# Four edits around an RWKV scan: the block inverse emitted ahead of its quarter, Gram products of both halves at once, the root of the first norm in PSUM, more filling ahead of chunk 0

## The chip, the cores and the metric

One core of a Trainium2 chip runs the whole program in one launch. TensorE (PE) does matrix products, VectorE (DVE), ScalarE (ACT) and GpSimd (POOL) do elementwise work, SyncE (SP) issues the transfers. The metric is device time in microseconds, the median of several executions.

## The reference

A trunk of two layers over 1024 tokens of width 1024, in float32. Layer 0 is an RMSNorm, one wide projection whose columns go to an RWKV-7 time mixer (8 heads of 64) and to chunked attention (8 heads of 64), gates, an output projection and a residual. Layer 1 is an RMSNorm, a projection, a gated position mixer and an output projection. A last RMSNorm follows. The part that the change touches most is the time mixer:

```python
def step(state, inp):
    r_t, w_t, k_t, v_t, a_t, b_t = inp
    sa = jnp.einsum('bhvk,bhk->bhv', state, a_t)
    state = (state * w_t[:, :, None, :]
             + sa[..., None] * b_t[:, :, None, :]
             + v_t[..., None] * k_t[:, :, None, :])
    y_t = jnp.einsum('bhvk,bhk->bhv', state, r_t)
    return state, y_t
...
y_a = rwkv7_mix(...) * jax.nn.silu(gate_a)
y_b = chunk_attention(q_b, k_b, v_b, att_bias) * jax.nn.silu(gate_b)
return h + jnp.concatenate([y_a, y_b], axis=-1) @ w_out
```

## The kernel before

A float32 product is done as three products of split operands (`mm3`, lines 262, 264, 266: high by high, high by low, low by high), which is the great bulk of TensorE's work; the high and low parts of the normed input are xH and xL, those of the weights wh and wl.

The stages in time:

- **Head** (to 36 us). x is loaded in eight tiles of 128 tokens, in two halves of four. `square` sums the squares; `scale0` forms the root with `rsqrt_act` (lines 89 to 93: reciprocal, square root on ScalarE, then three VectorE steps on tiles of four or two columns, in batches of 4, 2 and 2 tiles of x per half) and scales the tiles xt; `norm_t` transposes them (L305) and evicts xH (L307, ScalarE) and xL (L308, VectorE). GpSimd meanwhile makes the weights' low parts (L231). `lora_evac` follows the first projection and runs a Tanh (L452, with a load of ScalarE's function table) and two copies.
- **Projections** of the time mixer (36 to 255 us). They write ar, bk and v, the operands of the scan, to DRAM (`ar_d`, `bk_d`, `v_d`).
- **Scan** (about 263 to 560 us). 1024 tokens are 16 chunks of 64, in four quarters of four. `stage_a(q)` loads a quarter's operands (L691, L693, L696), forms the Gram products of keys and receptances per chunk and head (tile psg, L712), masks them into G and ag (L718, VectorE), scales bk (L675, GpSimd) and transposes it (pst, L681). A head pair stands in 128 partitions, head h in half h. `stage_b(q)` inverts the quarter's unit triangular blocks: four 32-wide transposes on VectorE (nw, L742), 15 times two small VectorE steps (L753, L755) on blocks of 16, and then four sets of 32-wide products on TensorE (psx, L771) with copies between, the last of them into G (L790). `stage_c(q)` runs the chain over chunks: zz and yy (L815, L818), copy z (L822), us (L825), copies uv (L828), us (L831), sum into the next chunk's uv (L836), yy (L838). `stage_d(q)` is the group norm of the result, with transposes psy (L872), and its store.
- **Filling.** Attention's projections (q, k, v, gate) are a generator of single matmuls. `fill.pump(n, mark, low)` emits n of them at a lowered priority, not ahead of the instruction mark. `QP`, `QB` and `QC` say how many go where: QP ahead of the first Gram product, QB[0] beside the first inverse, QB[q+1] between quarters, QC inside chunks. Their results leave by `split_evac` (tile hl, stored to q_d and k_d) and `vb_evac`.
- **Attention** (560 to 790 us), with the time mixer's output projection as filling (`out_steps`: residual tile res, loaded at L1135 from a pool of two buffers, summed at L1142, stored to hp_d at L1167), then attention's own half of the output projection.
- **Layer 1 and the last norm** (790 us to the end).

The order on every engine is set by the scheduler of the tile framework: it takes instructions by priority, which falls with the order of emission, and by its own estimate of readiness; `tc.add_manual_dep(..., sched_only)` adds an order without a semaphore. Within an engine everything then runs in that order.

Of the kernel before, what the change touches and what calls it, by code (L numbers as in the profile page):

```python
# [8 lines left out]
F32 = mybir.dt.float32  # L9
# [3 lines left out]
AF = mybir.ActivationFunctionType  # L13
# [39 lines left out]
YP = 1  # L53
LATE = 1
NPO = 1
QP = 44
FILLS = [5, 4, 4, 6, 4, 3, 3, 3]
QA = 14
QB = [80, 28, 16, 30]
QC = [[8, 8, 7], [8, 9, 7], [8, 8, 9], [8, 8, 7]]  # L60
W0SCALE = 0.6065306597126334

# [5 lines left out]
def rsqrt_small(nc, pool, out, v, tag):  # L68

    shp = list(v.shape)  # L70
    t = pool.tile(shp, F32, tag=tag, name="rsq_t")
    nc.vector.tensor_single_scalar(out.bitcast(I32), v.bitcast(I32), 1, op=ALU.arith_shift_right)
    nc.vector.tensor_scalar(out.bitcast(I32), out.bitcast(I32), -1, 0x5F3759DF, op0=ALU.mult, op1=ALU.add)
    if shp[1] == 1:
        h = pool.tile(shp, F32, tag=tag + "h", name="rsq_h")
        nc.vector.tensor_single_scalar(h, v, -0.5, op=ALU.mult)
    for _ in range(3):
        if shp[1] == 1:
            nc.vector.scalar_tensor_tensor(t, out, h, out, op0=ALU.mult, op1=ALU.mult)
        else:  # L80
            nc.vector.tensor_mul(t, out, out)
            nc.vector.scalar_tensor_tensor(t, t, -0.5, v, op0=ALU.mult, op1=ALU.mult)
        nc.vector.scalar_tensor_tensor(out, t, 1.5, out, op0=ALU.add, op1=ALU.mult)


def rsqrt_act(nc, pool, out, v):

    t = pool.tile(list(v.shape), F32, tag="rsqa", name="rsqa", bufs=2)
    nc.vector.reciprocal(t, v)
    nc.scalar.activation(out, t, AF.Sqrt)  # L90
    nc.vector.tensor_tensor(t, out, out, op=ALU.mult)
    nc.vector.scalar_tensor_tensor(t, t, -0.5, v, op0=ALU.mult, op1=ALU.mult)
    nc.vector.scalar_tensor_tensor(out, t, 1.5, out, op0=ALU.add, op1=ALU.mult)


@with_exitstack
def trunk_kernel(
# [13 lines left out]

    ident = cp.tile([P, P], F32, name="ident")
    make_identity(nc, ident)

    gmask = cp.tile([P, P], F32, name="gmask")
    nc.vector.memset(gmask, 1.0)
    for r in range(2):
        for q in range(2):
            blk = gmask[64 * r:64 * r + 64, 64 * q:64 * q + 64]
            nc.gpsimd.affine_select(  # L120
                out=blk, in_=blk, compare_op=ALU.is_ge, fill=0.0,
                base=-1 if q == 0 else 0, pattern=[[1, 64]], channel_multiplier=-1)
# [77 lines left out]
    def dtile(name, shape):  # L200
        return dr.tile(shape, F32, name=name)

    ya_d = dtile("ya_d", [NPAIR, P, T])
    yb_d = dtile("yb_d", [NPAIR, P, T])
    ar_d = dtile("ar_d", [NPAIR, P, 16, P])
    bk_d = dtile("bk_d", [NPAIR, P, 16, P])
    v_d = dtile("v_d", [NPAIR, T, P])
# [151 lines left out]
    def scale0(hf):  # L359
        for b in range(0, 4, BT[hf]):  # L360
            ts_ = range(4 * hf + b, 4 * hf + b + BT[hf])
            for t in ts_:
                square(t)
            bs = slice(ts_[0], ts_[-1] + 1)
            if any(SQ0[t] == "h" for t in ts_):
                nc.vector.tensor_tensor(ssq[:, 0, bs], ssq[:, 0, bs], ssq[:, 1, bs], op=ALU.add)
            nc.vector.tensor_scalar(ssq[:, 0, bs], ssq[:, 0, bs], 1.0 / D, 1e-6, op0=ALU.mult, op1=ALU.add)
            rsqrt_act(nc, p0, rstd[:, bs], ssq[:, 0, bs])
            for t in ts_:
                h_ = {"a": 1.0, "v": 0.0, "h": SPL}[SCL[t]]  # L370
                n_ = int(D * h_)
                if n_:
                    nc.scalar.mul(xt0[t][:, 0:n_], xt0[t][:, 0:n_], rstd[:, t:t + 1])
                if n_ < D:
                    nc.vector.tensor_scalar_mul(xt0[t][:, n_:D], xt0[t][:, n_:D], rstd[:, t:t + 1])
# [72 lines left out]
    def lora_evac(ps, hf):  # L448
        sh_wad(ps, hf)
        sl = slice(hf * 512, hf * 512 + 512)  # L450
        w, a = wad[hf][0:64], wad[hf][64:128]
        nc.scalar.activation(w, w, AF.Tanh)  # L452
        nc.scalar.copy(xw[0:64, sl], w)
        nc.scalar.copy(xa[64:128, sl], a)
# [90 lines left out]
    for p in range(NPAIR):  # L545
# [23 lines left out]
        for hf in range(2):  # L569
# [37 lines left out]
            nc.vector.tensor_tensor(kn, kn, ta, op=ALU.mult)  # L607
            nc.vector.tensor_tensor(bk[:, :, 0:64], c3(kn), c3(em), op=ALU.mult)
            nc.gpsimd.tensor_tensor(bk[:, :, 64:128], c3(km), c3(em), op=ALU.mult)
            nc.sync.dma_start(ar_d[p][:, 8 * hf:8 * hf + 8], ar)  # L610
            store_halves(bk_d[p][:, 8 * hf:8 * hf + 8], bk)
            def bonus(p=p, hf=hf, km=km, r=r, v=v, tsl=tsl):

                nc.vector.scalar_tensor_tensor(km, km, hrk[:, p:p + 1], r, op0=ALU.mult, op1=ALU.mult)
# [49 lines left out]
    def stage_a(q):  # L664
# [19 lines left out]
        for cg in range(2):  # L684
            o = 4 * q + 2 * cg
            uv = rq.tile([P, 2, 4, P], F32, tag="uv", name="uv", bufs=2)

            ag = rq.tile([P, 2, 4, 2, P], F32, tag="ag", name="ag", bufs=2)
            bk = (rb if q == 0 and cg else re_).tile(
                [P, 4, 2, P], F32, tag="bt" if q == 0 and cg else "bk", name="bk", bufs=2 if q == 0 and cg else 1)  # L690
            nc.sync.dma_start(bk, bk_d[:, :, o:o + 2, :].rearrange("a p c t -> p a c t"))  # L691
            for h in range(2):
                nc.sync.dma_start(ag[hss[h], h], ar_d[:, hss[h], o:o + 2, :].rearrange("a p c t -> p a c t"))  # L693
            for i in range(2):
                for h in range(2):
                    nc.sync.dma_start(  # L696
                        uv[oss[h], i, :, hss[h]],
                        v_d[:, 64 * (o + i):64 * (o + i) + 64, hss[h]].rearrange("a s n -> s a n"))
                    if q == cg == i == 0:
                        nc.gpsimd.memset(uv[hss[h], i, :, hss[h]], 0.0)  # L700
            if cg == 0:
                d["G"] = rq.tile([P, 2, 4, 2, P], F32, tag="G", name="G", bufs=1)
            g = d["G"][:, cg]
            bt = rq.tile([P, 4, 2, P], F32, tag="bt", name="bt", bufs=2)
            for pj in range(2):

                psg = [ps_m.tile([P, 4, P], F32, tag="m", name=f"psg{r}") for r in range(2)]
                for j in range(2):
                    for i in range(2):
                        for r in range(2):  # L710
                            for h in range(2):
                                nc.tensor.matmul(  # L712
                                    psg[r][(hss, oss)[r][h], 2 * j + i], lhsT=bk[hss[h], 2 * pj + j, i, (hss, oss)[r][h]],
                                    rhs=ag[hss[h], h, 2 * pj + j, i, :], start=True, stop=True)
                for dst, ps, r in ((g[:, 2 * pj:2 * pj + 2], psg[0], slice(0, P)),
                                   (ag[:, 0, 2 * pj:2 * pj + 2], psg[1], oss[0]),
                                   (ag[:, 1, 2 * pj:2 * pj + 2], psg[1], oss[1])):
                    nc.vector.tensor_tensor(  # L718
                        dst[r].rearrange("p j i t -> p (j i) t"), ps[r],
                        gmask[r].unsqueeze(1).to_broadcast([r.stop - r.start, 4, P]), op=ALU.mult)  # L720
# [395 lines left out]
    def out_steps(t, ps_o, src, k0, parts, resid, ht, hp, yp, yb_, hi=nc.scalar.copy, lo=nc.vector):  # L1116
# [81 lines left out]
    with tc.tile_pool(name="oh", bufs=1, reuse_waits="tile") as oh, \  # L1198
            tc.tile_pool(name="ps_ot", bufs=2, space=PSUM, reuse_waits="tile") as ps_ot:
        xss = []  # L1200
        for t in range(8):
# [185 lines left out]
```

## Time and profile before

| | us |
|---|---|
| median of 3 runs | 1215.05 (1209.55 to 1216.36) |
| the profiled execution | 1213.46 |
| its span, first to last instruction | 1211.7 |
| TensorE busy | 1132.9 (93%) |
| VectorE busy | 617.1 (51%) |
| ScalarE busy | 469.6 (39%) |
| GpSimd busy | 431.7 (36%) |
| mean granted TensorE clock | 0.962 of full speed |

The busy times are sums over a span of several stages with different limits, so each stage is read for itself. A row of the view by stretches gives, after the stretch and its length, the busy time of each engine with its count of instructions. In a row of the timeline the first number is the start, the second the time covered, xN the number of instructions run together, and the bracket says how long the engine stood idle before and what released it. A float32 matmul on TensorE leaves two records in the trace where the program has one instruction, so the trace counts 512 records of psg where the order has 256.

### The profile page before, as it was taken

To read this page: it belongs to the slowest core of one execution; us is meant where nothing else is said; L and a number is where in the kernel's file an instruction comes from. 1 tells how busy PE (TensorE), PEld (TensorE's weight loads), DVE (VectorE), ACT (ScalarE), POOL (GpSimd) and SP (SyncE) were. 2 spreads that over 40 slices of the span, in tenths; PEclk is the share of its full clock that TensorE was granted. 3 is DMA by queue.
4 is the path that set the end of the run, shared out by engine and by line. 5 is a ranking of instruction groups with operands and counts; after the bars stand their busy time and mean duration, and the time that the engine had idled before them with its cause. 6 is when DMAs were issued, how large, how long until landed. Compare 5 with 4: busy or idle time off the path is not lost.

```text
span 1211.7 us, 21587 instructions
## 1 busy us (share of the span) xinstructions
PE 1132.9 (93%) x8418; PEld 934.0 (77%) x8418; DVE 617.1 (51%) x1261; ACT 469.6 (39%) x1008; POOL 431.7 (36%) x447
## 2 busy tenths in 40 slices
PE   7899999979899798999998898799999999999997
PEld 4787778757767576777786777679999888888886
DVE  6555556547657649343677657265200463323443
ACT  5545554531323132223566645134425432221322
POOL 4335445342223323333322462311311464342232
PEclk8899999998999897999999899899999999999999
DMA  6115345477224441375577794764311132222542
GB/s 204 37 53 140 100 144 152 148 210 180 89 71 124 116 129 38 105 181 160 151 200 190 203 253 148 221 226 140 96 45 53 62 105 79 70 85 68 170 139 78
DMA packets 169127, 156.43 MB, mean 129 GB/s; under 512 B 25257, under 2 KB 138562, under 8 KB 168898
## 3 DMA queue, kind: packets, MB, share of 16 engines
q1 hardware_dynamic: 169026, 155.06, 43.8%
q8 instruction: 66, 1.08, 0.4%
q14 instruction: 35, 0.29, 0.1%
HBM read 102.02 MB, written 53.00 MB: 128 GB/s over the span
## 4 chain that ended last, share of the span: by engine, by line
PE 74%; DVE 11%; DMA 8%; issue 2%; ACT 2%; POOL 1%; SPq 1%; DVEq 0%; POOLq 0%; ACTq 0%
PE acc L262 13%; PE acc L264 13%; PE acc L266 13%; PE accv L262 3%; PE accv L264 3%; PE accv L266 3%; PE accu L262 2%; PE accu L264 2%; PE accu L266 2%; PE accg L262 2%; PE accg L266 2%; PE accg L264 2%; DMA res<-in_x_dram 1%; DVE nw L742 1%; PE st L1069 1%
## 5 line engine op out<-in xcount | busy, mean ns | idle before, releaser
L262 PE MATMUL acc<-xH,wh 128*128 128x512 f32 x528 | 215.1, 408 | 2.4 <-ACT xH L307 1.8
L264 PE MATMUL acc<-xL,wh 128*128 128x512 f32 x528 | 213.0, 404 | 0.0
L266 PE MATMUL acc<-xH,wl 128*128 128x512 f32 x528 | 211.8, 401 | 0.0
L231 POOL TENSOR_TENSOR wl<-wraw,wh 128x512 fp32r<-128x512 f32 (+1 forms) x106 | 149.4, 1429 | 166.0 <-ACT wh L228 156.0
L262 PEld LDWEIGHTS acc<-xH,wh 128*128 128x128 f32 x528 | 101.6, 192 | 24.6 <-ACT xH L307 2.2
L264 PEld LDWEIGHTS acc<-xL,wh 128*128 128x128 f32 x528 | 101.4, 192 | 21.6 <-issue 1.9
L266 PEld LDWEIGHTS acc<-xH,wl 128*128 128x128 f32 x528 | 101.1, 192 | 21.0 <-issue 0.3
L262 PE MATMUL acc<-WHL,yh 128*128 128x512 f32 x256 | 103.8, 405 | 13.0 <-DVE res L1142 7.2
L266 PE MATMUL acc<-WHL,yl 128*128 128x512 f32 x256 | 102.9, 402 | 0.0
L264 PE MATMUL acc<-WHL,yh 128*128 128x512 f32 x256 | 102.4, 400 | 0.0
L228 ACT CAST wh<-wraw 128x512 fp32r<-128x512 f32 (+1 forms) x102 | 62.4, 651 | 99.3 <-PE acc L264 38.3
L262 PE MATMUL accv<-wh,xH 128*128 128x256 f32 x256 | 72.2, 283 | 0.0
L264 PE MATMUL accv<-wl,xH 128*128 128x256 f32 x256 | 72.0, 283 | 0.0
L266 PE MATMUL accv<-wh,xL 128*128 128x256 f32 x256 | 71.6, 284 | 0.0
L262 PEld LDWEIGHTS acc<-WHL,yh 128*128 128x128 f32 x256 | 49.6, 194 | 24.2 <-issue 5.7
L266 PEld LDWEIGHTS acc<-WHL,yl 128*128 128x128 f32 x256 | 49.4, 193 | 10.4
L264 PEld LDWEIGHTS acc<-WHL,yh 128*128 128x128 f32 x256 | 49.6, 194 | 9.5
L1114 POOL TENSOR_TENSOR WHL<-wraw,WHL 128x512 fp32r<-128x512 f32 (+1 forms) x20 | 30.2, 1508 | 60.3 <-ACT WHL L1113 57.2
L262 PE MATMUL accu<-xH,wh 128*128 128x512 f32 x128 | 50.5, 395 | 0.0
L266 PE MATMUL accu<-xH,wl 128*128 128x512 f32 x128 | 49.9, 390 | 0.0
L264 PE MATMUL accu<-xL,wh 128*128 128x512 f32 x128 | 49.9, 390 | 0.0
L266 PE MATMUL accg<-xH,wl 128*128 128x512 f32 x128 | 49.9, 389 | 0.0
(430 smaller groups left out, 2463.8 us busy)
## 6 DMA issues: line engine op xcount, KB each, us to landing
wraw<-in_w_in_e_dram SPq DMA_DIRECT2D x66, 256.0 KB
wraw<-in_w_in_o_dram SPq DMA_DIRECT2D x32, 256.0 KB
xt<-in_x_dram SPq DMA_DIRECT2D x8, 512.0 KB
ar_d<-ar SPq DMA_DIRECT2D x8, 512.0 KB
q_d<-hl SPq DMA_DIRECT2D x8, 512.0 KB
bk<-bk_d SPq DMA_DIRECT2D x8, 512.0 KB
ag<-ar_d SPq DMA_DIRECT2D x16, 256.0 KB
bg<-bg_d SPq DMA_DIRECT2D x8, 512.0 KB
```

The costliest lines, as they stand in the source:

```text
L228: c_ = hi(wh[:, ks], raw)
L231: nc.gpsimd.tensor_tensor(wl[:, ks], raw, f32(wh[:, ks]), op=ALU.subtract)
L262: fill(nc.tensor.matmul(ps, lhsT=ah(k), rhs=bh(k), start=(k == 0), stop=False), k == 0)
L264: fill(nc.tensor.matmul(ps, lhsT=ah(k), rhs=bl(k), start=False, stop=False), False)
L266: fill(nc.tensor.matmul(ps, lhsT=al(k), rhs=bh(k), start=False, stop=(k == nk - 1)), False)
L742: mark = nc.vector.transpose(flat(nw[rs_]), g[rs_, :, o:o + 32].rearrange("p q (x t) -> p t x q", x=2))
L1069: nc.tensor.transpose(st[:, o:o + P], pfs[j][:, k0:k0 + P], ident)
L1114: (lo or (nc.vector if k % 2 else nc.gpsimd)).tensor_tensor(wl, raw, f32(wh), op=ALU.subtract)
```

## The change

1. `QP` goes from 44 to 84, `QB` from 80, 28, 16, 30 to 80, 10, 10, 10.
2. In the loop over quarters `stage_b(q + 1)` is emitted ahead of `stage_c(q)`, and the filling between quarters is tied to `stage_c`'s last copy.
3. The Gram product multiplies both 64-column halves of bk at once: 128 output partitions for one half of the input rows, so 8 instructions where 16 stood, in a tile psg for each input half. The masks become four of 64 partitions where one of 128 and two of 64 stood.
4. `rsqrt_act` can put the square root's result into PSUM, and its steps are arranged so that each reads the root from there; the head's batches do so. `rsqrt_small` for one column takes its operands as scalars by pointer.
5. The Tanh and two copies of `lora_evac` are ordered behind the eviction of xH that was emitted last.
6. `ar_d`, `bk_d` and `v_d` become two DRAM tiles each, one for each half of the tokens; the mask gmask is built by GpSimd just ahead of the scan; `res` has three buffers; the norm between the layers (`rms_scale`) takes its small tiles from another pool.

```diff
-QP = 44
+QP = 84
-QB = [80, 28, 16, 30]
+QB = [80, 10, 10, 10]
...
         if shp[1] == 1:
-            nc.vector.scalar_tensor_tensor(t, out, h, out, op0=ALU.mult, op1=ALU.mult)
+            nc.vector.tensor_scalar(t, out, h, out, op0=ALU.mult, op1=ALU.mult)
+            nc.vector.tensor_scalar(out, t, 1.5, out, op0=ALU.add, op1=ALU.mult)
...
-def rsqrt_act(nc, pool, out, v):
+def rsqrt_act(nc, pool, out, v, y=None):
     t = pool.tile(list(v.shape), F32, tag="rsqa", name="rsqa", bufs=2)
+    y = out if y is None else y
     nc.vector.reciprocal(t, v)
-    nc.scalar.activation(out, t, AF.Sqrt)
-    nc.vector.tensor_tensor(t, out, out, op=ALU.mult)
-    nc.vector.scalar_tensor_tensor(t, t, -0.5, v, op0=ALU.mult, op1=ALU.mult)
-    nc.vector.scalar_tensor_tensor(out, t, 1.5, out, op0=ALU.add, op1=ALU.mult)
+    nc.scalar.activation(y, t, AF.Sqrt)
+    nc.vector.scalar_tensor_tensor(t, v, -0.5, y, op0=ALU.mult, op1=ALU.mult)
+    nc.vector.tensor_tensor(t, t, y, op=ALU.mult)
+    nc.vector.scalar_tensor_tensor(out, t, 1.5, y, op0=ALU.add, op1=ALU.mult)
...
-            rsqrt_act(nc, p0, rstd[:, bs], ssq[:, 0, bs])
+            rsqrt_act(nc, p0, rstd[:, bs], ssq[:, 0, bs], ps_m.tile([P, BT[hf]], F32, tag="m", name="rsqp"))
...
-        nc.scalar.activation(w, w, AF.Tanh)
-        nc.scalar.copy(xw[0:64, sl], w)
-        nc.scalar.copy(xa[64:128, sl], a)
+        for i_ in (nc.scalar.activation(w, w, AF.Tanh), nc.scalar.copy(xw[0:64, sl], w),
+                   nc.scalar.copy(xa[64:128, sl], a)):
+            tc.add_manual_dep(i_.ins, evs[-1][0].ins.name, sched_only, reason="issue order")
...
-            nc.sync.dma_start(ar_d[p][:, 8 * hf:8 * hf + 8], ar)
-            store_halves(bk_d[p][:, 8 * hf:8 * hf + 8], bk)
+            nc.sync.dma_start(ar_d[hf][p], ar)
+            store_halves(bk_d[hf][p], bk)
...
-                psg = [ps_m.tile([P, 4, P], F32, tag="m", name=f"psg{r}") for r in range(2)]
+                psg = [ps_m.tile([P, 4, P], F32, tag="m", name=f"psg{h}") for h in range(2)]
                 for j in range(2):
                     for i in range(2):
-                        for r in range(2):
-                            for h in range(2):
-                                nc.tensor.matmul(
-                                    psg[r][(hss, oss)[r][h], 2 * j + i], lhsT=bk[hss[h], 2 * pj + j, i, (hss, oss)[r][h]],
-                                    rhs=ag[hss[h], h, 2 * pj + j, i, :], start=True, stop=True)
-                for dst, ps, r in ((g[:, 2 * pj:2 * pj + 2], psg[0], slice(0, P)),
-                                   (ag[:, 0, 2 * pj:2 * pj + 2], psg[1], oss[0]),
-                                   (ag[:, 1, 2 * pj:2 * pj + 2], psg[1], oss[1])):
-                    nc.vector.tensor_tensor(
-                        dst[r].rearrange("p j i t -> p (j i) t"), ps[r],
-                        gmask[r].unsqueeze(1).to_broadcast([r.stop - r.start, 4, P]), op=ALU.mult)
+                        for h in range(2):
+                            nc.tensor.matmul(psg[h][:, 2 * j + i], lhsT=bk[hss[h], 2 * pj + j, i, :],
+                                             rhs=ag[hss[h], h, 2 * pj + j, i, :], start=True, stop=True)
+                for h in range(2):
+                    for dst, r in ((g[:, 2 * pj:2 * pj + 2], hss[h]), (ag[:, h, 2 * pj:2 * pj + 2], oss[h])):
+                        nc.vector.tensor_tensor(
+                            dst[r].rearrange("p j i t -> p (j i) t"), psg[h][r],
+                            gmask[r].unsqueeze(1).to_broadcast([64, 4, P]), op=ALU.mult)
...
     for q in range(3):
-        stage_c(q)
+        stage_b(q + 1)
+        mark = stage_c(q)
         if q < 2:
             stage_a(q + 2)
-        fill.pump(QB[q + 1], stage_b(q + 1), FLB)
+        fill.pump(QB[q + 1], mark, FLB)
         stage_d(q)
...
-                xt = hp.tile([P, 512], F32, tag="res", name="res", bufs=2)
+                xt = hp.tile([P, 512], F32, tag="res", name="res", bufs=3)
```

What the edits move is seen in the order of instructions on an engine. (A row gives the line, the operation, and the tiles as out<-in; lines of the changed kernel are lower by 6 in the head and projections and by 1 from the Gram masks to the group norm, since lines were taken out or added above them.)

TensorE where the projections end and the scan begins, before: psb and psv are the last products of the projections, psg the first Gram products.

```order
L620 MATMUL psb<-kmh,bones 128x512
L629 MATMUL psv<-ident,vT 128x128 x4
L621 MATMUL psb<-kml,bones 128x512
L712 MATMUL psg_2500<-ag,bk 64x128
L712 MATMUL psg_2501<-ag,bk 64x128
```

Now, from the same psb; the filling that begins at L260 goes on for 39 matmuls in all behind psv before the Gram products come, four of one half and then four of the other:

```order
L614 MATMUL psb<-kmh,bones 128x512
L623 MATMUL psv<-ident,vT 128x128 x4
L260 MATMUL acc<-xH,wl 128x512
L615 MATMUL psb<-kml,bones 128x512
L256 MATMUL acc<-xH,wh 128x512
```

```order
L260 MATMUL acc<-xH,wl 128x512
L713 MATMUL psg_2566<-ag,bk 128x128 x4
L713 MATMUL psg_2567<-ag,bk 128x128 x4
L713 MATMUL psg_2580<-ag,bk 128x128 x4
L814 MATMUL zz<-uv,ag 64x64
```

So 39 filling matmuls moved in between, and a Gram tile takes four instructions where it took eight.

TensorE in chunks 1 and 2 of the first quarter, before: psx are the products of the next quarter's inverse, acc the filling.

```order
L266 MATMUL acc<-xH,wl 128x512
L771 MATMUL psx<-dt,G 32x32 x8
L825 MATMUL us<-z,G 64x64 x8
L262 MATMUL acc<-xH,wh 128x512
```

```order
L771 MATMUL psx<-dt,G 32x32 x10
L838 MATMUL yy<-uv,G 64x64
L771 MATMUL psx<-dt,G 32x32
L831 MATMUL us<-uv,bt 64x64 x8
L838 MATMUL yy<-uv,G 64x64 x7
```

Now, in chunk 2:

```order
L824 MATMUL us<-z,G 64x64 x8
L260 MATMUL acc<-xH,wl 128x512
L770 MATMUL psx<-dt,G 32x32 x64
L830 MATMUL us<-uv,bt 64x64 x8
L837 MATMUL yy<-uv,G 64x64 x8
```

The 64 products of the inverse's first set stand in one piece ahead of the chunk's second us, where they were spread over chunks in pieces of 1 to 20.

VectorE at chunk 0, before (nw is the start of the next quarter's inverse, uv the chunk's copies):

```order
L718 TENSOR_TENSOR G<-psg_2983,gmask 128x512
L718 TENSOR_TENSOR ag<-psg_2984,gmask 64x512 x2
L742 STREAM_TRANSPOSE nw<-G 32x512 x4
L828 COPY uv<-us 64x4x64
L745 SCALAR_TENSOR_TENSOR nb<-nw,half 128x256
L753 TENSOR_TENSOR nbt<-nq,nb 128x15
```

Now:

```order
L717 TENSOR_TENSOR G<-psg_3001,gmask 64x512
L717 TENSOR_TENSOR ag<-psg_3001,gmask 64x512
L741 STREAM_TRANSPOSE nw<-G 32x512 x2
L827 COPY uv<-us 64x4x64
L741 STREAM_TRANSPOSE nw<-G 32x512 x2
L835 TENSOR_TENSOR uv<-us,Sp 64x4x64 x2
```

The chunk's copy moved between two pairs of transposes.

ScalarE at the end of the head, before, and then now (wad is the tile of `lora_evac`):

```order
L373 ACTIVATE xt<-xt,rstd 128x1024
L452 ACT_TABLE_LOAD
L452 ACTIVATE wad<-wad 64x512
L454 CAST xa<-wad 64x512
L307 ACTIVATE xH<-pst,gcol 128x512 x3
```

```order
L367 ACTIVATE xt<-xt,rstd 128x1024
L301 ACTIVATE xH<-pst,gcol 128x512 x4
L222 CAST wh<-wraw 128x512
L301 ACTIVATE xH<-pst,gcol 128x512
L222 CAST wh<-wraw 128x512
L301 ACTIVATE xH<-pst,gcol 128x512 x3
L446 ACT_TABLE_LOAD
```

The table load moved behind all eight evictions of xH.

More of the change, by code (lines that the diff above doesn't have):

```diff
@@ L82, in rsqrt_small @@
             nc.vector.scalar_tensor_tensor(t, t, -0.5, v, op0=ALU.mult, op1=ALU.mult)
-        nc.vector.scalar_tensor_tensor(out, t, 1.5, out, op0=ALU.add, op1=ALU.mult)
-def rsqrt_act(nc, pool, out, v):
+            nc.vector.scalar_tensor_tensor(out, t, 1.5, out, op0=ALU.add, op1=ALU.mult)
+def rsqrt_act(nc, pool, out, v, y=None):
     t = pool.tile(list(v.shape), F32, tag="rsqa", name="rsqa", bufs=2)
+    y = out if y is None else y
     nc.vector.reciprocal(t, v)
-    nc.scalar.activation(out, t, AF.Sqrt)
-    nc.vector.tensor_tensor(t, out, out, op=ALU.mult)
-    nc.vector.scalar_tensor_tensor(t, t, -0.5, v, op0=ALU.mult, op1=ALU.mult)
-    nc.vector.scalar_tensor_tensor(out, t, 1.5, out, op0=ALU.add, op1=ALU.mult)
+    nc.scalar.activation(y, t, AF.Sqrt)
+    nc.vector.scalar_tensor_tensor(t, v, -0.5, y, op0=ALU.mult, op1=ALU.mult)
+    nc.vector.tensor_tensor(t, t, y, op=ALU.mult)
+    nc.vector.scalar_tensor_tensor(out, t, 1.5, y, op0=ALU.add, op1=ALU.mult)
 @with_exitstack
@@ L113, in trunk_kernel @@
     make_identity(nc, ident)
-    gmask = cp.tile([P, P], F32, name="gmask")
-    nc.vector.memset(gmask, 1.0)
-    for r in range(2):
[L118 to L122, printed above, removed]
     rows = [
@@ L204, in trunk_kernel @@
     yb_d = dtile("yb_d", [NPAIR, P, T])
-    ar_d = dtile("ar_d", [NPAIR, P, 16, P])
-    bk_d = dtile("bk_d", [NPAIR, P, 16, P])
-    v_d = dtile("v_d", [NPAIR, T, P])
+    ar_d = [dtile(f"ar_d{i}", [NPAIR, P, 8, P]) for i in range(2)]
+    bk_d = [dtile(f"bk_d{i}", [NPAIR, P, 8, P]) for i in range(2)]
+    v_d = [dtile(f"v_d{i}", [NPAIR, T // 2, P]) for i in range(2)]
     bg_d = dtile("bg_d", [NPAIR, 2, P, T])
@@ L631, in bonus @@
                 nc.scalar.copy(vt.rearrange("p a b -> p (a b)"), psv)
-                nc.sync.dma_start(v_d[p][tsl].rearrange("(a t) c -> t a c", t=P), vt)
+                nc.sync.dma_start(v_d[hf][p].rearrange("(a t) c -> t a c", t=P), vt)
             if p < NPAIR - 1 or hf == 0:
@@ L655, in trunk_kernel @@
     quart = [dict() for _ in range(4)]
+    gmask = rb.tile([P, P], F32, name="gmask")
+    nc.gpsimd.memset(gmask, 1.0)
+    for r in range(2):
+        for q in range(2):
+            blk = gmask[64 * r:64 * r + 64, 64 * q:64 * q + 64]
+            nc.gpsimd.affine_select(
+                out=blk, in_=blk, compare_op=ALU.is_ge, fill=0.0,
+                base=-1 if q == 0 else 0, pattern=[[1, 64]], channel_multiplier=-1)
     half = rb.tile([P, 2], F32, name="half")
@@ L690, in stage_a @@
                 [P, 4, 2, P], F32, tag="bt" if q == 0 and cg else "bk", name="bk", bufs=2 if q == 0 and cg else 1)
-            nc.sync.dma_start(bk, bk_d[:, :, o:o + 2, :].rearrange("a p c t -> p a c t"))
+            nc.sync.dma_start(bk, bk_d[o // 8][:, :, o % 8:o % 8 + 2, :].rearrange("a p c t -> p a c t"))
             for h in range(2):
-                nc.sync.dma_start(ag[hss[h], h], ar_d[:, hss[h], o:o + 2, :].rearrange("a p c t -> p a c t"))
+                nc.sync.dma_start(ag[hss[h], h], ar_d[o // 8][:, hss[h], o % 8:o % 8 + 2, :].rearrange("a p c t -> p a c t"))
             for i in range(2):
@@ L697, in stage_a @@
                         uv[oss[h], i, :, hss[h]],
-                        v_d[:, 64 * (o + i):64 * (o + i) + 64, hss[h]].rearrange("a s n -> s a n"))
+                        v_d[o // 8][:, 64 * (o % 8 + i):64 * (o % 8 + i) + 64, hss[h]].rearrange("a s n -> s a n"))
                     if q == cg == i == 0:
@@ L1210, in trunk_kernel @@
             xss.append(oh.tile([P, D], F32, tag="xs", name="xs", bufs=XSB))
-            rms_scale(oh, ht, xss[t])
+            rms_scale(cp, ht, xss[t])
             if t % 4 == 3:
```

1 line of the change is left out of this document (removed).

## The prediction

> **What bounds the kernel now.** I read the span and the busy time by stage first, then TensorE's waits, then the chain that ended last around each long wait, then single rows. The columns of the second view are: stretch, its length, busy us (and instructions) of each engine, granted TensorE clock, DMA share, GB/s.
>
> ```profile
> span 1211.7 us, 21587 instructions
> 260.00:290.00 30.00, 20.85 (x201) 16.75 (x200) 13.88 (x19) 4.65 (x8) 10.70 (x19) 0.77 1.03 221
> 290.00:340.00 50.00, 42.73 (x730) 33.96 (x729) 35.66 (x84) 15.49 (x30) 11.95 (x14) 0.95 0.36 109
> 340.00:380.00 40.00, 40.00 (x638) 30.33 (x637) 20.07 (x46) 10.49 (x22) 10.66 (x14) 0.98 0.36 100
> 380.00:410.00 30.00, 24.52 (x335) 18.94 (x333) 28.52 (x54) 6.74 (x13) 12.96 (x12) 0.89 0.28 84
> 410.00:450.00 40.00, 36.48 (x513) 27.90 (x513) 16.09 (x34) 9.72 (x21) 12.12 (x16) 0.96 0.47 127
> 450.00:490.00 40.00, 34.52 (x545) 26.91 (x544) 32.73 (x74) 11.05 (x23) 13.07 (x13) 0.83 0.31 93
> 790.00:1190.00 400.00, 400.00 (x2215) 349.29 (x2214) 150.68 (x303) 136.52 (x307) 131.52 (x84) 1.00 0.32 101
> ```
>
> TensorE (first busy column) is the bound, and full from 790 to 1190, so nothing is to be had there. What is open lies in the scan: 9.2 us idle from 260 to 290, then 7.3, 0, 5.5, 3.5 and 5.5, together 21.7 from 290 to 490, where the clock falls to 0.89 and 0.83 in the stretches in which VectorE (third column) is nearly full: 28.52 of 30. The longest waits of TensorE, with total us, times, longest:
>
> ```profile
> PE psg L712 <- DMA ag<-ar_d: 11.1, 3, 7.7
> PE pst L305 <- DVE xt L375: 7.5, 3, 4.4
> PE acc L262 <- DVE res L1142: 7.2, 3, 4.8
> PE us L825 <- DVE z L822: 5.6, 3, 2.2
> PE psy L872 <- DVE G L790: 3.4, 3, 2.8
> PE us L831 <- DVE uv L828: 2.7, 1, 2.7
> ```
>
> The first, the two on a chunk's copies (z, uv) and the one on the inverse's last copy (G L790) are the scan's; L305 is the head's, L1142 the attention's. Each has an edit against it.
>
> **The head (root in PSUM, Tanh held back).** The chain that ended last, before the projections start:
>
> ```profile
> 28.86 1.16 DVE rsqa L91
> 30.05 1.23 DVE rsqa L92
> 31.30 0.17 DVE rstd L93
> 31.56 1.15 ACT xt L373
> 32.72 1.28 ACT L452
> 34.02 0.63 ACT wad L452
> 34.67 0.61 ACT xa L454
> 36.05 0.80 PE acc L262
> ```
>
> and beside it on GpSimd, from the timeline:
>
> ```profile
> 30.00 1.25 POOL L231 TENSOR_TENSOR wl<-wraw,wh 128x512 fp32r<-128x512 f32 x1
> ```
>
> Two root steps on tiles of two columns take 1.2 us each, while GpSimd subtracts weight tiles (one of them shown), where L93 on the same shape takes 0.17 once that is done. With the root in PSUM each step keeps one SBUF input; I take 0.2 for each, so 2 us less. Behind that, ScalarE loads Tanh's table (1.28) and does two pieces (1.24) ahead of the last xH evictions that the second half's matmuls wait for; put behind them, that is 2.5 less, and the transposes' turn is nearer. From 36.05 I take 5 off. Bounds: 2, if the steps are still held, and 6. The Trainium skill, "SBUF — State Buffer", section "Who interferes with whom", says that a VectorE instruction with two SBUF inputs contends with a GpSimd one that reads SBUF and that one with at most one does not; the rows above (1.2 us beside GpSimd) agree, and by it the root term would be the full one.
>
> **40 more filling matmuls ahead of the scan; split DRAM tiles.** SyncE issues the scan's first loads at 265.33, and the first Gram product starts at 271.12:
>
> ```profile
> 265.33 0.44 SPq L691 DMA_DIRECT2D bk<-bk_d  x1
> 271.12 0.69 PE L712 MATMUL psg<-ag,bk 64*64 64x128 f32 x4 [7.69 <-DMA ag<-ar_d]
> 285.22 0.66 PE L681 MATMUL pst<-ident,bk 128*128 128x128 f32 x4
> 258.43 0.23 PE acc L266
> ```
>
> A filling matmul takes 0.23 (0.228 over longer runs), so the 39 that now stand between the last projection product and the first Gram product take 8.9 and cover the 7.7 of waiting. On SyncE these loads now stand behind a second store of q, whose eviction follows the 48th filling matmul; 36 are left then, 8.2 us, against some 2 for eviction and issue and 5.8 (271.12 less 265.33) for the loads: just covered. The Gram section behind it took 14.1 (271.12 to 285.22) with masks on VectorE setting the pace; 16 masks of 0.69 now give 11 to 11.5. So 7.7 + 14.1 = 21.8 becomes 20.4, with 9.1 us of filling done that is missing later. The quotas take 40 fillings from later and 4 more fall out of the scan into attention (+0.9). Net 9.6 less; bounds 1 (the wait stays) and 11.
>
> **Gram products of both halves at once.** The groups by line and shape:
>
> ```profile
> L712 PE MATMUL psg<-ag,bk 64*64 64x128 f32 x512 | 35.0, 301 | 14.7 <-DMA ag<-ar_d 11.1 <-DVE G L718 1.9 <-DMA bk<-bk_d 1.1
> L718 DVE TENSOR_TENSOR ag<-psg,gmask 64x512 f32<-64x512 f32 x32 | 22.0, 689 | 7.0 <-PE psg L712 6.4
> L712 PEld LDWEIGHTS psg<-ag,bk 64*64 64x64 f32 x512 | 25.6, 146 | 22.0 <-issue 12.9 <-DMA ag<-ar_d 4.2 <-DVE G L718 2.5
> L681 PEld LDWEIGHTS pst<-ident,bk 128*128 128x128 f32 x64 | 7.7, 149 | 4.9 <-issue 2.7 <-POOL bk L675 0.8 <-ACT bt L682 0.6
> ```
>
> 512 records become 256, in 16 groups. A group takes 2.2 now (35.0 over 16). The transposes with 128 columns at 285.22 are 0.12 apart (0.66 less one duration of 0.30, over three), so 16 records at that spacing take 1.9, and 1.0 if the two halves overlap in pairs; the order puts four products of one half and then four of the other in many groups, which speaks for 1.9. For the 12 groups of the later quarters that is 4 to 15 less, and nothing if the loads set the pace; I take 5, near the 1.9. The price is on VectorE: 64 masks of 0.689 for 32 of 0.689 and 16 of 0.686 at full height, 11 us more, 2.8 in a quarter. The Trainium skill, "TensorE: Matmul & The Clock Gate", section "LDWEIGHTS (loading the stationary operand)", has the load's time go by columns, so half as many loads of twice the columns would save nothing, and the sum would be 5 higher. The two load rows above speak against it: 146 ns with 64 columns, 149 with 128.
>
> **Inverse ahead of the quarter.** Two quarters, from the first us product of chunk 0 to those of chunks 4 and 8, and the transposes that begin the inverse of quarter 1:
>
> ```profile
> 323.20 0.30 PE L825 MATMUL us<-z,G 64*64 64x64 f32 x2
> 325.85 4.21 DVE L742 STREAM_TRANSPOSE nw<-G 32x512 f32<-32x512 f32 x4
> 396.90 0.91 PE L825 MATMUL us<-z,G 64*64 64x64 f32 x12
> 471.26 1.11 PE L825 MATMUL us<-z,G 64*64 64x64 f32 x14
> ```
>
> So 73.7 and 74.4 us. The inverse of quarter 1 begins at 325.85, but its 32-wide products are strewn among four chunks at low priority and the last copy into G comes only shortly before 396.90, where chunk 4 waits (the wait on G L790 above, 2.8 the longest). Afterwards they stand whole in chunks 2 and 3, and the four transposes of 4.2 us, behind which uv waited (2.7), stand in two pairs around that copy. Of the 21.7 idle I let 15.5 go (the waits on z, uv and G above are 11.7 of it; the rest is what follows from them) and put 4.5 back: a product of the inverse now stands in TensorE's order in chunk 2, and if VectorE is late with 30 steps, everything behind it waits, where before it slid. The lost clock: busy time from 290 to 490 times what the clock lacks is 42.7 x 0.05 + 40.0 x 0.02 + 24.5 x 0.11 + 36.5 x 0.04 + 34.5 x 0.17, about 13; with fewer holes I give 7 back. Scan: 11 + 7 + 5 (Gram) = 23 less; bounds 8 (half of the idle, no clock) and 38.
>
> **Third residual buffer.** The chain in attention:
>
> ```profile
> 765.85 4.00 DMA hp_d<-res
> 769.87 6.92 DMA res<-in_x_dram
> 777.82 0.76 PE acc L262
> ```
>
> The load of a residual tile waits for the store out of the same buffer (two of them), and TensorE stands 4.8 us at 777.82. A third buffer starts the load two tiles earlier; of the 7.2 waited on L1142 I take 6; bounds 0 and 10 (clock included). What is late next is the store itself, covered by the next tile's 24 matmuls of 0.23.
>
> The small root with pointer scalars, the scale's pool and the later mask tile lie beside full TensorE stretches; if not, each is under 1 us.
>
> **Sum.** 1213.5 (span 1211.7 and 1.8 around it; the median of the runs is 1.6 above) - 5 - 9.6 - 23 - 6 = 1169.9: **1170**.
>
> **Rivals.**
> *Cover missing.* The loads stay stuck on SyncE, or the Gram products cost the same: 5 to 9 back, 1175 to 1179 and with both 1184. For it: 8.2 of cover against 7.8.
> *VectorE becomes the scan's bound.* It is in order, has 2.8 us more per quarter, and chunk copies stand behind mask pairs (1.4) or transpose pairs (2.1). If each of 36 copies loses 0.6 net of its cover of 7 to 8 fillings (1.8), 21 come back: 1191. For it: 28.52 of 30 from 380 to 410. Against: 16 to 20 of 40 beside it.
> *Slower.* The inverse now leads, and its 30 steps per quarter, with two SBUF inputs, run beside GpSimd. Fifteen of the 30, alone and then in a crowded stretch:
>
> ```profile
> 284.00:303.00 19.00, 3.09 (x15) 1.00 0.58 161
> 388.00:412.00 24.00, 5.72 (x15) 0.86 0.31 94
> ```
>
> That is 0.21 and 0.38 each. The kernel is no faster when 90 steps cost 43.6 more, a mean of 0.69; at 0.8 it is 1213 + 10 = 1223. Single rows of 1.2 exist, a mean over 0.38 doesn't, so a small chance.
> *The change doesn't act.* The order shows that all parts stand; only covers could fail everywhere at once.
>
> **How the numbers follow.** My forecast, 1157 to 1183, has 0.55; missing cover (up to 1184) 0.17; VectorE bound (1183 to 1205) 0.19; no difference 0.04; slower 0.05. Half a per cent, 6 us, is what a measurement can tell from no change. The range of 8 in 10, 1152 to 1196, takes the first two and most of the third; its lower end is the better bounds of the Gram and the idle. Faster 0.91, same 0.04, slower 0.05.
>
> **What would show it.** Projections start near 31 and the table load stands behind xH; no wait of 7.7 at the first Gram product, and chunk 0 starts near 317 instead of 323 with 40 more fillings done; the first two quarters at about 50 and 60 us; psg's busy time near 25; no 4.8 at the residual. I am wrong if TensorE stands at the inverse's products in chunks 2 and 3, if psg keeps 35 us, or if z and uv wait longer in total than now.

## The result, and the profile after

The changed kernel takes 1180.0 us (median of 4 runs, 1178.2 to 1185.6), the kernel before 1215.6 beside it: ratio 0.9726, 95% interval 0.968 to 0.9771. The forecast was 1170 within 1152 to 1196, so direction and range hold and the gain is 35.6 us where 43.6 was forecast. The profiled execution has a span of 1178.6 us. Its stages, in the columns used above (stretch, length, busy us of each engine, granted clock, DMA share, GB/s); the four quarters now begin at 329.4, 382.3, 445.3 and 504.1:

```profile
span 1178.6 us, 21117 instructions
255.00:270.00 15.00, 11.15 (x55) 9.05 (x53) 2.26 (x4) 3.54 (x6) 6.70 (x20) 1.00 1.02 264
270.00:290.00 20.00, 18.75 (x103) 16.38 (x102) 13.69 (x20) 1.17 (x2) 4.08 (x4) 0.50 1.00 197
290.00:310.00 20.00, 17.80 (x81) 14.23 (x80) 16.14 (x41) 4.69 (x9) 2.98 (x4) 0.81 0.29 90
330.00:382.00 52.00, 48.04 (x839) 37.76 (x837) 36.26 (x75) 14.47 (x31) 15.63 (x21) 1.00 0.31 89
382.00:445.00 63.00, 59.23 (x919) 46.88 (x918) 47.35 (x107) 19.02 (x39) 24.56 (x28) 0.97 0.45 123
445.00:504.00 59.00, 54.02 (x866) 42.30 (x864) 40.33 (x91) 18.33 (x39) 24.63 (x28) 0.94 0.33 100
```

The first three quarters of the kernel before, for comparison:

```profile
323.00:397.00 74.00, 65.06 (x999) 49.96 (x994) 52.05 (x105) 20.35 (x42) 23.01 (x26) 0.93 0.33 94
397.00:470.00 73.00, 64.40 (x972) 49.66 (x972) 45.74 (x94) 18.17 (x38) 22.73 (x26) 0.90 0.35 99
470.00:529.00 59.00, 55.18 (x843) 42.91 (x842) 30.51 (x75) 16.50 (x35) 22.65 (x26) 0.96 0.31 97
```

The first two quarters are 21 and 10 us shorter, near the 50 and 60 us that were forecast, with the clock at 1.00 and 0.97 for 0.93 and 0.90. The third is as long as before. What strikes is the clock at the start: 0.50 from 270 to 290, where the Gram products are; before it was 0.76 from 271 to 290. TensorE's waits that answer to those of before:

```profile
PE psg L713 <- DMA ag<-ar_d: 3.8, 1, 3.8
PE pst L299 <- DVE xt L369: 3.5, 2, 3.1
PE acc L256 <- DVE res L1142: 3.4, 2, 3.2
PE us L830 <- DVE uv L827: 3.1, 4, 1.2
PE psy L871 <- DVE G L789: 2.4, 1, 2.4
```

The wait on z is gone, that on uv is four short ones, the residual's is halved. The stages, each between two products of TensorE, in us (the forecast has 40 filling matmuls, 9.1 us, moved from the third line into the second):

| from, to | before | after | change | forecast |
|---|---|---|---|---|
| start, last projection product (psb) | 263.4 | 256.5 | -6.9 | -5 |
| then to us of chunk 0 | 59.8 | 72.9 | +13.1 | -1.4 |
| chunk 0 to chunk 15 | 236.7 | 209.9 | -26.8 | -32.1 |
| chunk 15 to layer 1 | 261.2 | 248.5 | -12.7 | -5.1 |
| layer 1 to the last product | 383.2 | 383.3 | +0.1 | 0 |
| sum | | | -33.2 | -43.6 |

So the miss of 10 is a miss of 14.5 in the second line and of 5.3 in the third, of which the first and the fourth make up 9.5. The second line in the timeline of the changed kernel: the 48th filling matmul, ScalarE's eviction of its result (q), and SyncE's store of q and first load of the scan:

```profile
256.84 0.40 PE L260 MATMUL acc<-xH,wl 128*128 128x512 f32 x1
259.08 0.59 ACT L884 ACTIVATE hl<-acc 128x512 fp32r<-128x512 f32 x1
260.74 0.39 SPq L886 DMA_DIRECT2D q_d<-hl  x1
261.71 1.28 SPq L694 DMA_DIRECT2D bk<-bk_d  x1
```

The forecast had some 2 us for eviction and issue behind the 48th filling matmul and 5.8 for the loads. Eviction and issue took 4.5 (257.24 to 261.71): the eviction starts 1.8 us after the matmul ends, behind a cast on ScalarE that waited for a weight tile's load, and the store of q is issued behind another store, of bg at 260.31. The loads took 7.5 (261.71 to 269.25, where the first Gram product starts), with a DMA share of 1.02. So the fillings end 3.85 too early, the clock goes to half, and the Gram section lasts until 286.29, 17.0 us where 11.5 was forecast.

### The profile page after: what moved, and what is told of

It reads as the page before. It is cut to its first block, busy times and chain, and to the rows that moved or that the text cites. A ratio compares the mean times of both kernels' runs of the same rounds, so it can differ in the third digit from the quotient of the medians.

```text
span 1178.6 us, 21117 instructions
## 1 busy us (share of the span) xinstructions
PE 1119.8 (95%) x8162; PEld 929.2 (79%) x8162; DVE 622.6 (53%) x1276; ACT 469.0 (40%) x1008; POOL 432.0 (37%) x448
## 4 chain that ended last, share of the span: by engine, by line
PE 58%; DMA 7%; DVE 5%; ACT 1%; issue 1%; POOL 1%; SPq 0%; DVEq 0%; ACTq 0%; POOLq 0%
PE acc L256 8%; PE acc L258 8%; PE acc L260 8%; PE accv L256 3%; PE accv L260 3%; PE accv L258 3%; PE accu L256 3%; PE accu L260 2%; PE accg L260 2%; PE accu L258 2%; PE accg L258 2%; PE accg L256 2%; PE st L1069 2%; DMA wraw<-in_w_out_e_dram 2%; PE psx L770 1%; PE psg L713 1%
## 5 line engine op out<-in xcount | busy, mean ns | idle before, releaser
L260 PE MATMUL acc<-xH,wl 128*128 128x512 f32 x528 | 212.0, 401 | 0.0
L260 PEld LDWEIGHTS acc<-xH,wl 128*128 128x128 f32 x528 | 101.0, 191 | 21.2
L256 PE MATMUL acc<-WHL,yh 128*128 128x512 f32 x256 | 101.9, 398 | 4.5 <-DVE res L1142 3.4
L258 PE MATMUL acc<-WHL,yh 128*128 128x512 f32 x256 | 100.8, 394 | 0.0
L260 PE MATMUL acc<-WHL,yl 128*128 128x512 f32 x256 | 100.8, 394 | 0.0
L260 PE MATMUL accv<-wh,xL 128*128 128x256 f32 x256 | 71.4, 285 | 0.0
L256 PEld LDWEIGHTS acc<-WHL,yh 128*128 128x128 f32 x256 | 48.4, 189 | 15.6 <-DVE res L1142 4.1
L258 PEld LDWEIGHTS acc<-WHL,yh 128*128 128x128 f32 x256 | 48.3, 189 | 9.6 <-POOL WHL L1114 0.2
L260 PEld LDWEIGHTS acc<-WHL,yl 128*128 128x128 f32 x256 | 48.1, 188 | 9.7
L260 PE MATMUL accu<-xH,wl 128*128 128x512 f32 x128 | 49.9, 390 | 0.0
L260 PE MATMUL accg<-xH,wl 128*128 128x512 f32 x128 | 49.9, 389 | 0.0
L256 PE MATMUL accg<-xH,wh 128*128 128x512 f32 x128 | 49.8, 389 | 0.0
```

The source lines that it names most:

```text
L256: fill(nc.tensor.matmul(ps, lhsT=ah(k), rhs=bh(k), start=(k == 0), stop=False), k == 0)
L258: fill(nc.tensor.matmul(ps, lhsT=ah(k), rhs=bl(k), start=False, stop=False), False)
L260: fill(nc.tensor.matmul(ps, lhsT=al(k), rhs=bh(k), start=False, stop=(k == nk - 1)), False)
```

## The experiments

Nine kernels take one part of the change away or add to it, three go on from the best of them. Times are medians; ratios are to the kernel before, run beside them.

**More filling ahead, 108 and 132.** Does the wait cost the clock, or the new Gram products?

```diff
-QP = 84
+QP = 108
```

> The changed kernel with 24 more filling matmuls ahead of the first Gram product (QP 108 for 84). Theory: the 3.9 us for which TensorE stands before the first Gram product, because the loads land late, is what halves the clock, and the half clock until 294 us is what the first stretch lost. Then the wait goes, the clock stays at 1.00 from 260 to 300 us, the Gram section takes about 11.5 us for 17, chunk 0 starts near 321 us for 329 with 24 more fillings done, and the time is 1164 to 1170. Rival: the Gram products themselves (64 rows, one half after the other) let the clock fall; then only the wait goes, the clock is 0.50 in the Gram section all the same, and the time is about 1176.

Measured: 1174.9 us, 0.9673 (0.9639 to 0.9706). A wait of 1.55 us was left, up to 274.12, inside the Gram products. Four stretches of TensorE (length, busy, clock, DMA share, GB/s):

```profile
268.00:272.00 4.00, 4.00 (x26) 1.00 1.23 194
272.00:276.00 4.00, 2.45 (x24) 0.84 1.14 224
276.00:280.00 4.00, 4.00 (x26) 0.50 1.20 204
292.00:296.00 4.00, 4.00 (x15) 0.60 0.67 193
```

The clock falls all the same and comes back after 292, as the rival expected. But the wait that is left may have done it, so this doesn't decide it:

```diff
-QP = 84
+QP = 132
```

> The changed kernel with 48 more filling matmuls ahead of the first Gram product (QP 132). With 108 a wait of 1.6 us was left inside the Gram products and the clock was 0.50 from 275 to 293 us. If the wait starts it, this kernel, without a wait, keeps 1.00 and takes 11.5 us for the Gram section, 1164 to 1168. If the new products themselves let it fall, the clock goes to 0.50 within some 8 us of their start without any wait and comes back only with the next filling, and the time stays near 1175.

Measured: 1173.0 us, 0.968 (0.9653 to 0.9707). No wait is left ahead of the Gram products or in them, and the clock stays up:

```profile
268.00:272.00 4.00, 4.00 (x30) 1.00 1.22 240
272.00:276.00 4.00, 4.00 (x26) 1.00 1.23 196
276.00:280.00 4.00, 4.00 (x51) 1.00 1.22 203
280.00:284.00 4.00, 2.24 (x18) 1.00 0.86 194
284.00:288.00 4.00, 1.06 (x5) 0.65 1.02 311
288.00:292.00 4.00, 4.00 (x11) 0.50 1.07 306
```

and in its timeline:

```profile
286.94 1.11 PE L896 MATMUL pv<-ident,vs 128*128 128x128 f32 x4 [4.70 <-ACT vs L893]
```

So the products don't bring the clock down without a wait, and their section takes 12.2 us at full clock (270.06 to 282.24, where the last product ends), near the 11 to 11.5 of the masks' pace. By the same measure it took 16.5 in the changed kernel. The forecast time of 1164 to 1168 still failed: a new wait of 4.7 us stands right behind, on the filling's own staging (vs), and takes the clock there. The Trainium skill, "TensorE: Matmul & The Clock Gate", section "HAM oscillation — how this bites in real kernels", gives gaps over some 3.4 us as those that bring the clock down. The waits of 3.85 and 4.70 agree; in the kernel with 108 the clock came down behind a wait of 1.55, with Gram products before and after it. So a shorter wait is enough here, and the measurement decides.

**Gram products as before.**

```diff
-                        for h in range(2):
-                            nc.tensor.matmul(psg[h][:, 2 * j + i], lhsT=bk[hss[h], 2 * pj + j, i, :],
+                        for r in range(2):
+                            for h in range(2):
+                                nc.tensor.matmul(
+                                    psg[r][(hss, oss)[r][h], 2 * j + i], lhsT=bk[hss[h], 2 * pj + j, i, (hss, oss)[r][h]],
...
```

> The changed kernel with the Gram products and masks as before (two output halves apart, 16 products a pair of heads). Theory: the new form costs clock at the start and saves in the later quarters; with the old form the clock comes back near 280 us as it did before the change, chunk 0 starts about 5 us earlier, the later three quarters are 5 to 8 longer together, the time is 1178 to 1184. Rival 1, as predicted: no effect at the start, later quarters 5 longer, 1185. Rival 2, loads go by columns: no difference anywhere but 11 us less on VectorE, time 1175 to 1180.

Measured: 1169.3 us, 0.9624 (0.9594 to 0.9653): 10.7 us faster than the whole change, which none of the three readings had. Its clock, after nearly the same wait (3.75 us), and then that of the changed kernel:

```profile
272.00:276.00 4.00, 3.15 (x31) 0.50 1.20 225
276.00:280.00 4.00, 4.00 (x48) 0.59 1.24 200
280.00:284.00 4.00, 3.93 (x65) 1.00 1.18 193
```

```profile
276.00:280.00 4.00, 4.00 (x28) 0.50 1.23 191
280.00:284.00 4.00, 4.00 (x27) 0.50 1.04 189
288.00:292.00 4.00, 3.95 (x12) 0.50 0.39 127
292.00:296.00 4.00, 4.00 (x19) 0.75 0.01 4
```

With the old products the clock is back at 280, inside the Gram section; with the new ones only at 294, when the next filling has run for 5 us. The old form has a wait of its own later, 4.75 us on vs before 300, and still comes out ahead. Chunk 0 starts at 324.9 for 329.4, and chunk 0 to 15 takes 204.0 for 209.9. The products themselves, at full clock, the old form and then the new (rows of the timelines of this kernel and of the one with 132; groups of records without other work between):

```profile
408.15 1.10 PE L714 MATMUL psg<-ag,bk 64*64 64x128 f32 x32 [0.26 <-DMA uv<-v_d]
389.09 1.09 PE L714 MATMUL psg<-ag,bk 64*64 64x128 f32 x16
```

```profile
270.06 1.17 PE L713 MATMUL psg<-ag,bk 64*128 64x128 f32 x16
274.10 1.16 PE L713 MATMUL psg<-ag,bk 64*128 64x128 f32 x8
```

A group of a head pair is 32 records in the old form and 16 in the new. In the better order, in one piece, the old group takes 1.10 and the new one 1.17; in two pieces each takes about twice that, 1.09 or 1.16 a piece. Since 32 records take no longer than 16, the two output halves must have run side by side already; doing them in one instruction saves nothing. In sum psg is busy 33.7 us here and 34.2 in the changed kernel.

**Is it the masks?** The old products, with 16 more masks (11 us more on VectorE):

```diff
-                for dst, ps, r in ((g[:, 2 * pj:2 * pj + 2], psg[0], slice(0, P)),
+                for dst, ps, r in ((g[:, 2 * pj:2 * pj + 2], psg[0], hss[0]),
+                                   (g[:, 2 * pj:2 * pj + 2], psg[0], hss[1]),
```

> The changed kernel with the Gram products as before but four masks of 64 rows for one of 128 and two of 64, so 16 masks and 11 us more on VectorE. Theory: of the 10.7 us that the old form is faster, some 6 are these masks, in the quarters, and the rest is the clock at the start: 1173 to 1177. Rival: VectorE has room, all of it was clock and order: 1168 to 1171.

Measured: 1178.1 us, 0.9712 (0.9679 to 0.9745), 8.9 slower than without them, the intervals apart; 6 was expected. Three quarters without (from 325, 380, 446) and with them (from 326, 386, 455), third busy column VectorE:

```profile
325.00:380.00 55.00, 53.00 (x942) 41.34 (x943) 36.75 (x80) 16.26 (x34) 17.66 (x22) 0.97 0.31 92
380.00:446.00 66.00, 60.76 (x983) 46.89 (x982) 45.87 (x106) 18.80 (x39) 25.57 (x28) 0.97 0.46 131
446.00:498.00 52.00, 47.59 (x878) 37.56 (x878) 32.10 (x71) 15.85 (x34) 19.96 (x24) 1.00 0.38 108
```

```profile
326.00:386.00 60.00, 54.57 (x890) 40.92 (x886) 37.78 (x78) 15.69 (x33) 17.18 (x22) 0.94 0.30 85
386.00:455.00 69.00, 59.64 (x1001) 47.01 (x1003) 49.07 (x112) 18.97 (x39) 23.08 (x27) 0.95 0.41 112
455.00:511.00 56.00, 50.99 (x879) 39.77 (x870) 35.89 (x74) 16.18 (x35) 22.60 (x27) 0.94 0.38 107
```

Each quarter is 3 to 5 longer with TensorE's clock lower, though VectorE is busy for only two thirds of it. From 325 to 545 TensorE's waits add up to 19.9 us for 11.3: 6.6 for none on bk, which GpSimd scales, 5.5 for 3.9 on masked tiles (ag), 1.8 for 0.7 on the inverse's copies. That all of this comes of masks standing ahead of other work on VectorE, which runs in order, is an inference. The scheduler also shifts other instructions when masks are added, so not every microsecond is theirs.

With the masks alike, the two forms of product can't be told apart in the total: 1178.1 here with the old products, 1180.0 in the changed kernel with the new ones. In their profiles the old ones start chunk 0 at 326.1 for 329.4 and then take 215.4 for 209.9 to chunk 15; whether that second difference is the products' or comes of shifted instructions is open. The clock came back at 280 to 284 here too, so the masks are not what holds it down at the start; the products' form is. Why, is open: one half's 64 rows at a time would fit, and no run shows it.

**Order as before.**

```diff
-        stage_b(q + 1)
-        mark = stage_c(q)
+        stage_c(q)
         if q < 2:
             stage_a(q + 2)
-        fill.pump(QB[q + 1], mark, FLB)
+        fill.pump(QB[q + 1], stage_b(q + 1), FLB)
```

> The changed kernel with the inverse emitted behind the quarter as before, quotas as changed. Theory: this edit carries most of the gain in the scan; from chunk 0 to chunk 15 it takes 20 us more than the 210 of the changed kernel, waits on z, uv and the last copy into G come back, the time is about 1200. Rival: the quotas carried it, and the order gives 5 to 10: 1185 to 1190.

Measured: 1209.5 us, 0.9967 (0.9942 to 0.9993): undoing the order loses 29.5 of the 35.6 us, more than the 20 that were expected. Chunk 0 to 15 takes 237.8 us, as in the kernel before (236.7), and waits of this kind are back:

```profile
PE us L824 <- DVE z L821: 6.5, 2, 4.0
PE psx L770 <- DVE dt L782: 4.4, 1, 4.4
PE psy L871 <- DVE G L789: 2.6, 2, 2.4
PE psg L713 <- DVE ag L717: 2.3, 3, 1.3
```

**Filling quotas as before** (QP 44, QB 80, 28, 16, 30).

> The changed kernel with the filling as before (QP 44, QB 80, 28, 16, 30). Theory: the 40 fillings moved ahead earned little, since the wait was only half covered and the clock fell all the same: 1180 to 1186, with a wait of 6 to 8 us before the first Gram product, chunk 0 some 10 us earlier and the quarters some 10 longer together. Rival, as predicted: they pay 9.6, about 1190.

Measured: 1181.5 us, 0.9732 (0.9697 to 0.9767), not to be told from the whole change. The first wait is 9.5 us for 3.85 and chunk 0 starts 6.4 earlier; chunk 0 to 15 is 8.2 longer. The 40 fillings were moved, not hidden. Here no second store of q stands ahead of the loads, the only one goes out 3.0 us before them, as in the kernel before, and the loads still take 7.6 us (256.99 to 264.55). So a store right ahead is not needed for slow loads.

**The head, two parts.**

```diff
-            rsqrt_act(nc, p0, rstd[:, bs], ssq[:, 0, bs], ps_m.tile([P, BT[hf]], F32, tag="m", name="rsqp"))
+            rsqrt_act(nc, p0, rstd[:, bs], ssq[:, 0, bs])
```

> The changed kernel with the head's root in SBUF again (its steps in the new order). Theory: steps on four and two columns take up to 1.2 us beside GpSimd for 0.15, several of them on the way to the scaled tiles; the projections end 3 to 4 us later, time about 1183. Rival: the steps stand beside other work, less than 1 us.

Measured: 1183.1 us, 0.9762 (0.9731 to 0.9793); the last projection product ends at 260.3 for 256.5, so 3.8 later. Two root steps with the root in SBUF, and the same two in the changed kernel, both while GpSimd subtracts weight tiles:

```profile
29.16 1.22 DVE L94 SCALAR_TENSOR_TENSOR rsqa<-ssq,rstd 128x2 f32<-128x2 f32 x1
30.41 1.23 DVE L95 TENSOR_TENSOR rsqa<-rsqa,rstd 128x2 f32<-128x2 f32 x1
```

```profile
26.46 0.14 DVE L94 SCALAR_TENSOR_TENSOR rsqa<-ssq,rsqp 128x2 f32<-128x2 f32 x1
26.64 0.16 DVE L95 TENSOR_TENSOR rsqa<-rsqa,rsqp 128x2 f32<-128x2 f32 x1
```

In the second edit the Tanh and its copies are issued without the dependency, as before the change.

> The changed kernel with the Tanh and its table load free to go ahead of the last xH evictions. Theory: the head's 6.9 us are 3.8 of the root and 3.1 of this; the projections end 3 us later, time about 1183. Rival: the second half's evictions hide it, 1180.

Measured: 1186.3 us, 0.978 (0.9748 to 0.9812); the projections end 3.7 later. Together 7.5, against the 6.9 by which the head is shorter. In the totals both kernels' intervals overlap that of the whole change, so the two parts rest on their profiles.

**Two residual buffers** (`bufs=2` for res).

> The changed kernel with two buffers for the residual tile again. Theory: attention and its projections, 12 us shorter than before, owe most of that to the third buffer; with two the waits on the residual add come back (7 us before, the clock with them) and the time is 1187 to 1190. Rival: attention is shorter since fewer of its fillings were left over for it or since it met its data earlier; then 1180 to 1182.

Measured: 1193.5 us, 0.9859 (0.9824 to 0.9893). The profiled execution is the fastest of the five, 1187.4; there attention to layer 1 takes 245.7 us for 238.7. VectorE's wait for the residual's load is 13.6 us, for 7.2 in the changed kernel and 16.9 before; TensorE's wait on the sum grows from 3.4 to 4.2:

```profile
DVE res L1142 <- DMA res<-in_x_dram: 13.6, 4, 6.4
PE acc L256 <- DVE res L1142: 4.2, 3, 3.6
```

TensorE also waits 2.4 us for the other tile of that line (ht), which it doesn't do in the changed kernel. So its waits there grow by 3.2 of the 7; the rest goes with a busy time that is 4 us longer in the stage, at a clock of 0.97 for 0.98. The buffer is worth 7 in the profile and 13 in the medians; what the four slower executions wait for was not seen.

**From the best kernel on.** The old Gram products with QP 120:

> The changed kernel with the Gram products and masks as before and QP 120. Theory: with the old form the clock is only lost to the wait ahead of it (3.75 us at QP 84); covered, the clock stays at 1.00, the Gram section takes 11 us for 15.5, and 1169 becomes 1160 to 1164. Rival: the old form too lets the clock fall (64 rows), then only the wait goes and 1165 to 1167 come out; or the fillings are then missing in the chunks and it is 1169 to 1173.

Measured: 1173.2 us, 0.9676 (0.9646 to 0.9706). The clock stays at 1.00 up to 284, but a wait of 6.5 us on vs stands at 288. Then the stores of the filling's q, k and v moved from SyncE's queue to ScalarE's (`nc.scalar.dma_start` in `split_evac` and `vb_evac`):

> The kernel with the old Gram products (1169) whose filling results q, k and v are stored from ScalarE's queue, not SyncE's. Theory: TensorE's wait of 4.75 us at 300 us for a filling's staging buffer comes of a store that stands behind 28 loads of the scan in SyncE's order; from another queue it goes at once and 3 to 6 us are won: 1163 to 1167. Rival: ScalarE now waits with the store for VectorE and holds up the chunk's copies, or its issues cost as much: 1169 to 1174.

Measured: 1182.0 us, 0.9766 (0.9723 to 0.9808). The profiled execution is the slowest of the four, 1189.8. In it the wait on vs is gone, which fits the store's place in SyncE's order as its cause; but others take its place, the first Gram product's 5.5 us and those of the chunks:

```profile
PE psg L714 <- DMA ag<-ar_d: 5.9, 2, 5.5
PE us L833 <- DVE uv L830: 2.5, 2, 2.1
PE us L827 <- DVE z L824: 2.2, 1, 2.2
```

The same with QP 104:

> The same with QP 104. Theory: the filling's stores out of the way, more filling ahead covers the wait of 3.75 us before the first Gram product and the clock stays up, 1159 to 1163. Rival: the 20 fillings are missing later as they were with QP 120, where 1169 became 1173: 1167 to 1172.

Measured: 1179.0 us, 0.9729 (0.9701 to 0.9756). Both are slower than the kernel they start from, where 1163 to 1167 and 1159 to 1163 were expected. That one, the change with the old Gram products, has the lowest median of all: 1169.3.

## Why the prediction was right or wrong

- **Sum.** The range held, but that the total came within 10 us is in part luck: errors in both directions offset each other. Two terms failed outright (filling, Gram products); the order, the head and the residual buffer gave more than forecast.
- **Head, 5 less.** Right, and 6.9 in all. The matmuls go on without a break from 31.18 for 36.05, so 4.9 of it stand there as forecast; behind that the clock from 36 to 60 us is 1.00 for 0.89, which the forecast left out. The steps beside GpSimd fell from 1.2 to 0.15 as the rule on SBUF inputs in the Trainium skill ("SBUF — State Buffer", "Who interferes with whom") has it. Undone, each of the two parts costs 3.7 to 3.8, where 2 and 2.5 were forecast.
- **Filling ahead, 9.6 less.** Wrong: 1.5, within the interval. The failing step is "just covered". "Some 2 for eviction and issue" was 4.5, since other work stood ahead of them in ScalarE's and SyncE's order; the loads' 5.8, read from the profile before, were 7.5. The longer loads are not due to the store of q right ahead of them (the kernel with the old quotas has 7.6 without it); their cause is open. The 3.85 left halved the clock, and the step "11 to 11.5" for the Gram section held only without that wait (12.2 in the kernel with 132). The rival named "cover missing" came true: 8.1 of the 9.6 did not come, within its 5 to 9. It priced the wait and not the clock behind it.
- **Gram products, 5 less.** Wrong, in sign: the edit costs 10.7, of which 8.9 are its masks (next point), so the products themselves give nothing that shows in the total. A sign of being wrong that was on record came: psg is busy 34.2 us, where near 25 was forecast. The term took 2.2 us for an old group from a mean of 35.0 over 16 groups, which mixes both orders and stretches at half clock. An old group in its better order takes 1.10, a new one 1.17. The rule on weight loads that the prediction set aside (the Trainium skill, "TensorE: Matmul & The Clock Gate", "LDWEIGHTS (loading the stationary operand)") gave the right result, nothing saved. It is not shown to be the reason: median loads are 133 ns with 64 columns and 188 with 128, so longer, though not twice.
- **VectorE.** The 2.8 us of masks per quarter were noted as a price and then left out of the sum; they cost 8.9 with the old products. This is the rival "VectorE becomes the scan's bound", in part: not by its busy share, and, as far as the waits tell, by what stands behind the masks.
- **Inverse ahead, 11 idle and 7 clock.** Right and too small: undone, it costs 29.5, and chunk 0 to 15 is 27.9 longer. In that kernel the quotas of 10 between quarters stayed, so some of the 29.5 may be theirs with the old order; that was not taken apart.
- **Third residual buffer, 6 less.** Right and too small: 7 to 13, of which TensorE's waits at the sums are 3.2. Of the 12.7 in that line 7 are thus shown; where the other 5 to 6 come from is open.
- **The rival on the other side,** 30 steps held by GpSimd, did not come: chunk 0 to 15 is 27 shorter.

## What to carry to other kernels

Before merging small matmuls into fewer, look whether they already run side by side: compare the time of a whole group at full clock, not the count nor a mean over stretches at full and at half clock. Where a transfer is to be covered, time the whole way to its issue, with what stands ahead of it on each engine, and not the transfer alone. On an engine that works in order, price added instructions by what stands behind them, even where the engine is a third idle. A wait that is covered almost is worth little: what is left of it may cost the clock for several times its length: here 3.85 us were left, and the clock was at half for 24.

## What the runs showed of the hardware

- At full clock 32 Gram records with 64 output columns took 1.10 us, and 16 with 128 columns 1.17; in the poorer order 16 took 1.09 and 8 took 1.16.
- A TensorE that is busy without a gap can stay at a clock of 0.50: in the changed kernel from 272 to 284 us (4.00 of 4.00 busy in each stretch by the profile). It was back at 294, 5 us after the large matmuls had begun; in the kernel with the old quotas it was back at 289, 4 us after they had. With the old products it was back about 10 us after the first one.
- A wait of 1.55 us among such products was enough to bring the clock from 1.00 to 0.50; in the kernel with QP 132, without that wait, it stayed at 1.00. In the last kernel (old products, QP 104) it went to 0.50 behind a wait of 1.82 ahead of the first product.
